# Three chained transformer blocks: kept products before two norms, a second router on unscaled rows, and block 3's biases, values and key weights on other queues

## The chip, the cores and the metric

One NeuronCore of one Trainium2 chip runs the whole program; the other cores are idle. The time is device microseconds of one execution. Shown are 3 runs of the kernel before, and one more execution under the hardware profiler, which gives the trace. TensorE is PE below, VectorE DVE, ScalarE ACT, GpSimd POOL and SyncE SP.

## The reference

Sequence 512, width 1024, batch 1, everything in float32. Block 1 is a hybrid mixer, a cross attention on 512 memory rows and a hierarchical mixture of experts; block 2 has differential, window and memory attention on one projection and an expert-choice feed-forward; block 3 has neighbourhood and latent attention and a SwiGLU. What the change touches, cut to the core:

```
def rms_norm(x, gain):
    return x * lax.rsqrt(jnp.mean(x * x, -1, keepdims=True) + EPS) * gain

def expert_choice_ffn(h, w_router, w_gate, w_up, w_down):   # h = rms_norm(x, ffn_norm_g_2)
    aff = jax.nn.softmax(h @ w_router, axis=-1)             # 512 x 16
    g, idx = lax.top_k(swapaxes(aff, 1, 2), cap)            # the 64 best rows of each expert
    xe = h[idx]
    ye = (silu(xe @ w_gate) * (xe @ w_up)) @ w_down         # 16 experts
    return zeros_like(h).at[idx].add(ye * g[..., None])

def memory_attention(q, mk, mv):                            # block 2
    return softmax(q @ mk.T * scale) @ mv

def neighbourhood_attention_2d(q, k, v, rpb):               # block 3: 8 rows x 64 columns, 8 heads
    s = q @ k_nb.T * scale + rpb_cols[:, row_bias_idx]      # bias by the distance in rows and columns
    return softmax(s) @ v_nb
```

## The kernel before, in words

It is one program for one core, written with tile pools; a scheduler orders each engine's instructions when the program is built, and inserts the waits. Nothing is reordered at run time: an instruction that waits holds up all behind it on its engine, and a DMA issue that waits holds up its engine's queue.

A float32 product is made of three fast ones: each operand is split into a high part (wh, xh: a cast on ACT, line 218) and a low part (wl, xl: a subtraction on DVE, line 221), and PE adds high by high, low by high and high by low. Weights come in groups of 4 x 128 rows by 512 columns (raw, 1 MB) through SP's queue (raw_group, line 340). dense_tiles (line 367 issues its matmuls) works through the four token tiles of 128 rows for a first use; dense (line 419) holds four accumulators and runs over k.

*out_proj* (line 282) runs token tiles 0 and 1, then 2 and 3. In each pass it goes over k, splits two halves of 512 output columns, and multiplies for both tiles in turn. Both tiles of a pass so end together; finish then adds to the residual h (line 311) and calls the norm of the next step.

*Block 2's router* (moe2_tile, router_T, line 883 on): DVE multiplies the residual by the norm's gain (L883, 128x512 twice a tile), PE transposes (L433), copies go to SBUF (L438, L436), PE multiplies by the router weights (L894), and the softmax takes the row factor r in. The transposed affinities (L1582) of four tiles then go through 8 rounds of MAX8 and MATCH_REPLACE on DVE (L1594, L1595), 8 rows of each expert a round. Beside each round keep_warm issues one small matmul and 5 of 128x128 on PE (L191, L193). From the replaced places the positions follow (L1600 to L1604), PE transposes them (L1607), DVE builds one-hot tiles, PE gathers each expert's rows (L1625), and the experts run (L1662 gate and up, L1693 down), with weights streamed into all free room. For each pair of experts two broadcasts of positions and affinities (L1669) serve the later scatter.

*Block 2's memory attention* consists of parts of two heads and 256 queries: scores (L828) into PSUM, softmax on DVE and ACT (L456 to L476), transposes (L836), copies (L839), and for every two parts value products (L1393). The scheduler puts them between the matmuls of block 2's projections (L419).

*Block 3's neighbourhood attention* (mixer3): values v are projected first (line 1765), written row tile by row tile to DRAM (vd, L1766) and read back in eight windows (vw, L1785). Queries and keys follow. The position bias is read as overlapping rows (rv, L1794), which come mirrored; a matmul with the anti-diagonal matrix turns them (L1797), and DVE adds the mask (L1802). The vd, vw and rv transfers are on ACT's queue, between its casts.

## Time and profile before

| what | value |
|---|---|
| median of 3 runs | 3418.66 us (3416.3 to 3419.46) |
| profiled execution | 3424.08 us |
| its span | 3422.2 us |
| TensorE clock granted, mean | 0.983 |
| PE / DVE / ACT / POOL busy | 95% / 48% / 38% / 4% |
| DMA moved | 713.96 MB, mean 209 GB/s |

Busy shares are averages over stages with different limits, and a busy PE is modelled from issue to end, so back-to-back matmuls show longer than their spacing. The profiled execution is 5.4 us above the median of the runs. [...]

### The profile page before, as it was taken

How to read it: one execution, taken by the hardware profiler on the slowest of the kernel's cores; microseconds unless marked ns; L12 is line 12 of the kernel's file. 1: busy time of each engine (PE TensorE's matmuls, PEld its weight loads, DVE VectorE, ACT ScalarE, POOL GpSimd, SP SyncE). 2: the span in 40 equal slices, each digit the busy share in tenths (PEclk: the TensorE clock that was granted, in tenths of full speed). 3: DMA queues.
4: the chain of work that ended last, by engine and by line, in shares of the span. 5: the costliest groups of instructions: out<-in, count | busy, mean ns of one | idle time of the engine just before them, and what ended most of it. 6: DMA issues, size and time to landing. Idle time of an engine off the chain costs nothing.

```text
span 3422.2 us, 41346 instructions
## 1 busy us (share of the span) xinstructions
PE 3242.2 (95%) x15500; PEld 2092.0 (61%) x15500; DVE 1636.8 (48%) x3520; ACT 1289.1 (38%) x2662; POOL 130.4 (4%) x128
## 2 busy tenths in 40 slices
PE   8999989998999999999999998898888999999998
PEld 6777866667767767668634333232224676788886
DVE  5546789998354454656311111011014446573356
ACT  6334658886344353554100000000003344452244
POOL 0010010002000000000000000000000000000000
PEclk9999989999999999999899999999999999999999
DMA  5115479985112212114799999999997312133243
GB/s 169 58 62 141 148 261 376 373 313 199 62 50 72 73 53 87 50 35 171 269 402 420 422 420 422 421 421 423 420 422 272 98 50 68 62 99 99 80 165 137
DMA packets 212938, 713.96 MB, mean 209 GB/s; under 512 B 20144, under 2 KB 28096, under 8 KB 180352
## 3 DMA queue, kind: packets, MB, share of 16 engines
q1 hardware_dynamic: 190272, 668.38, 51.1%
q10 hardware_dynamic: 19520, 32.43, 3.0%
q0 software_dynamic: 2944, 10.49, 1.0%
q8 instruction: 123, 2.02, 0.2%
q14 instruction: 79, 0.65, 0.1%
HBM read 693.68 MB, written 17.56 MB: 208 GB/s over the span
## 4 chain that ended last, share of the span: by engine, by line
PE 75%; DMA 13%; DVE 6%; ACT 2%; issue 1%; POOL 1%; ACTq 0%; SPq 0%; POOLq 0%; DVEq 0%
PE acc L419 23%; PE acc L1662 8%; PE acc L282 7%; PE acc L1085 5%; PE acc L1277 5%; PE acc L1693 3%; PE acc L1107 2%; PE pst L433 2%; DMA xl<-in_w_exp_up_dram 2%; DMA rawx<-in_w_exp_gate_dram 2%; DMA xl<-in_w_exp_down_dram 2%; PE sc L1625 2%; PE acc L367 2%; DMA rawx<-in_w_exp_down_dram 2%; DVE wl L221 1%
## 5 line engine op out<-in xcount | busy, mean ns | idle before, releaser
L221 DVE TENSOR_TENSOR wl<-raw,wh 128x512 fp32r<-128x512 f32 (+3 forms) x910 | 606.6, 683 | 578.0 <-ACT wh L218 525.1
L218 ACT CAST wh<-raw 128x512 fp32r<-128x512 f32 (+3 forms) x910 | 546.5, 612 | 737.8 <-PE acc L419 491.4
L419 PE MATMUL acc<-xh,wh 128*128 128x512 f32 x1072 | 426.4, 398 | 7.1 <-ACT wh L218 5.0
L419 PE MATMUL acc<-xl,wh 128*128 128x512 f32 x1072 | 425.0, 396 | 0.0
L419 PE MATMUL acc<-xh,wl 128*128 128x512 f32 x1072 | 424.4, 396 | 0.0
L1662 PE MATMUL acc<-rawx,xe 128*64 128x512 f32 x1256 | 293.0, 601 | 29.3 <-DMA rawx<-in_w_exp_up_dram 20.9
L419 PEld LDWEIGHTS acc<-xh,wh 128*128 128x128 f32 x1072 | 202.2, 189 | 61.0 <-issue 10.2
L419 PEld LDWEIGHTS acc<-xl,wh 128*128 128x128 f32 x1072 | 202.4, 189 | 51.5 <-issue 13.2
L419 PEld LDWEIGHTS acc<-xh,wl 128*128 128x128 f32 x1072 | 202.2, 189 | 50.4 <-issue 10.8
L1662 PEld LDWEIGHTS acc<-rawx,xe 128*64 128x64 f32 x1256 | 84.2, 137 | 228.2 <-issue 147.7
L1693 PE MATMUL acc<-rawx,wh 128*64 128x512 f32 x640 | 147.0, 599 | 13.1 <-DMA rawx<-in_w_exp_down_dram 13.0
L282 PE MATMUL acc<-wl,xsh 128*128 128x512 f32 x336 | 132.9, 396 | 4.8 <-DVE wl L221 4.7
L207 POOL TENSOR_TENSOR pw_r<-pw_v,halfneg 128x1 f32<-128x1 f32 (+2 forms) x64 | 58.4, 913 | 2053.8 <-DVE pw_v L206 2036.2
L282 PE MATMUL acc<-wh,xsl 128*128 128x512 f32 x336 | 132.2, 394 | 0.0
L282 PE MATMUL acc<-wh,xsh 128*128 128x512 f32 x336 | 128.7, 392 | 0.0
L1662 PE MATMUL acc<-raw,xe 128*64 128x512 f32 x512 | 119.2, 598 | 9.6 <-DMA raw<-in_w_exp_gate_dram 9.6
L1681 DVE SCALAR_TENSOR_TENSOR wl<-wl,acc 128x512 f32<-128x512 f32 x32 | 22.0, 687 | 205.0 <-PE acc L1662 205.0
L468 ACT ACTIVATE e<-e,smx 128x512 f32<-128x512 f32 (+3 forms) x160 | 98.7, 618 | 50.1 <-DVE smx L466 37.3
L438 ACT COPY wh<-pst 128x512 f32<-128x512 f32 x32 | 18.7, 585 | 260.1 <-PE pst L433 260.0
L1693 PEld LDWEIGHTS acc<-rawx,wh 128*64 128x64 f32 x640 | 42.1, 136 | 103.7 <-issue 68.5
L1085 PE MATMUL acc<-wh,xeh 128*96 128x512 f32 x256 | 103.6, 406 | 0.7 <-ACT xeh L218 0.7
L1085 PE MATMUL acc<-wl,xeh 128*96 128x512 f32 x256 | 103.6, 404 | 0.0
(538 smaller groups left out, 5581.3 us busy)
## 6 DMA issues: line engine op xcount, KB each, us to landing
rawx<-in_w_exp_up_dram SPq DMA_DIRECT2D x80, 1024.0 KB
rawx<-in_w_exp_down_dram SPq DMA_DIRECT2D x80, 1024.0 KB
rawx<-in_w_exp_gate_dram SPq DMA_DIRECT2D x77, 1024.0 KB
raw<-in_w_in_dram SPq DMA_DIRECT2D x58, 1024.0 KB
raw<-in_w_exp_gate_dram SPq DMA_DIRECT2D x34, 1024.0 KB
raw<-in_w_exp_down_dram SPq DMA_DIRECT2D x32, 1024.0 KB
raw<-in_w_exp_up_dram SPq DMA_DIRECT2D x30, 1024.0 KB
raw<-in_w_ffn_out_dram SPq DMA_DIRECT2D x22, 1024.0 KB
```

The lines of the kernel that those rows point to most:

```text
L218: nc.scalar.copy(hi, src)
L221: nc.vector.tensor_sub(lo, src, hi.bitcast(F32))
L282: nc.tensor.matmul(acc[a, hf], l[:, js], r, start=(k == 0 and q == 0), stop=(k == nk - 1 and q == 2))
L367: self.nc.tensor.matmul(acc[a], l[:, k, js], r[:, :n], start=(k == 0 and q == 0), stop=(k == nk - 1 and q == 2))
L419: nc.tensor.matmul(outs[j], l, r, start=(kk == 0 and q == 0), stop=(kk == nk - 1 and q == 2))
L433: nc.tensor.transpose(pt[:, k * P:(k + 1) * P], src[:, (b + k) * P:(b + k + 1) * P], self.ident)
L468: nc.scalar.activation(es[i], src[i], AF.Exp, bias=nm[:, i:i + 1], scale=sc[i], accum_out=l[:, i:i + 1])
L1085: nc.tensor.matmul(ps, l[:, k], r, start=(k == 0 and q == 0), stop=(k == 7 and q == 2))
L1107: nc.tensor.matmul(py[hf], l[:, k], r, start=(k == 0 and q == 0), stop=(k == 3 and q == 2))
L1277: nc.tensor.matmul(acc[j], l[:, js], r, start=(k == 0 and q == 0), stop=(k == nk - 1 and q == 2))
L1662: nc.tensor.matmul(acc[f // 2][f % 2 * 64:(f % 2 + 1) * 64], cur[:, k, es], raw[f], start=(k == 0), stop=(k == 7))
L1693: nc.tensor.matmul(py[hf * 64:(hf + 1) * 64], uT[ab][:, kk, c * 64:(c + 1) * 64], raw[:, d, hf * 512:(hf + 1) * 512], start=(i + d == 0), ...
```

## The change

1. out_proj gets keep=True for w_out (block 1) and w_out_2 (block 2): in the pass of tiles 2 and 3, the products of the last two k are held back, and issued for tile 2, then for tile 3, each right ahead of that tile's finish.
2. Block 2's router transposes h itself. The norm's gain is multiplied into the router weights once, at the start of the program: a new load fgain (128x8x1 of float32, from ffn_norm_g_2) stands on ACT's queue behind the load of those weights, and a new DVE multiply (line 1353 of the changed kernel) waits for both. The scaled rows hn (ACT, h times r) are written after the router; the gathered rows xe are multiplied by the gain where they were copied. The load of the gain as a full row goes.
3. The last of the 8 top-k rounds issues 1 matmul to keep PE busy, in place of 5.
4. The first pair's broadcasts (L1669) are issued behind expert 0's gate products.
5. The mirrored bias is written once to DRAM (rpb_d) by eight DRAM-to-DRAM copies on SP's queue, early in block 2, behind a weight load; rv is read from there, already turned, and the anti-diagonal matmul and its matrix go. rv, vd and vw are issued from POOL. The key weights (columns 512 to 1023) are loaded ahead into the room of the later merged tile, and the weights of values and queries are loaded ahead too.

The diff, cut:

```
@@ -262,7 +262,7 @@
-    def out_proj(self, W, nk, get, upd, after):
+    def out_proj(self, W, nk, get, upd, after, keep=False):
@@ -270,18 +270,30 @@
+            kept = []
...
+            def products(a, k, hf, x, w):
+                js = slice((a - tiles[0]) * P, (a - tiles[0] + 1) * P)
+                for q, (l, r) in enumerate(((0, 0), (0, 1), (1, 0))):
+                    nc.tensor.matmul(acc[a, hf], x[l][:, js], w[r], start=(k == 0 and q == 0),
+                                     stop=(k == nk - 1 and q == 2))
...
                     raws[k // 2] = load(k)
-                xh, xl = get(k, tiles[0] * P)
+                x = get(k, tiles[0] * P)
                 for hf in range(2):
-                    wh, wl = self.wsplit(raws[k // 2][:, k % 2, hf * 512:(hf + 1) * 512], 512)
-                    for i, a in enumerate(tiles):
-                        js = slice(i * P, (i + 1) * P)
-                        for q, (l, r) in enumerate(((xh, wh), (xh, wl), (xl, wh))):
-                            nc.tensor.matmul(acc[a, hf], l[:, js], r, start=(k == 0 and q == 0),
-                                             stop=(k == nk - 1 and q == 2))
+                    w = self.wsplit(raws[k // 2][:, k % 2, hf * 512:(hf + 1) * 512], 512)
+                    if keep and tiles[0] and k >= nk - 2:
+                        kept.append((k, hf, x, w))
+                    else:
+                        for a in tiles:
+                            products(a, k, hf, x, w)
...
             def finish(a):
+                for b in kept:
+                    products(a, *b)
                 for hf in range(2):
@@ -342,7 +354,7 @@
-        self.nc.sync.dma_start(v, W[k0 * P:(k0 + g) * P, c0:c0 + n].rearrange("(g p) n -> p g n", p=P))
+        self.loaded = self.nc.sync.dma_start(v, W[k0 * P:(k0 + g) * P, c0:c0 + n].rearrange("(g p) n -> p g n", p=P)).ins
@@ -784,7 +796,7 @@
         self.out_proj(I["w_out"], 8, lambda k, t0: (yh[:, k, t0:t0 + 256], yl[:, k, t0:t0 + 256]), self.add_h,
-                      lambda a: self.norm_tile(a, g, yh, yl))
+                      lambda a: self.norm_tile(a, g, yh, yl), keep=True)
         return yh, yl
@@ -1337,6 +1349,8 @@
         nc.scalar.dma_start(self.rw, I["w_router_2"].rearrange("(k p) e -> p k e", p=P))
+        nc.scalar.dma_start(self.fgain, I["ffn_norm_g_2"].rearrange("o (k p) -> p (o k)", p=P))
+        nc.vector.tensor_mul(self.rw, self.rw, self.fgain.unsqueeze(2).to_broadcast([P, 8, 16]))
         Q = lambda: B.tile([P, S], F32, name="qkv", bufs=24)
@@ -1366,6 +1380,15 @@
+        self.rpb_d = self.dr.tile([8, P, 489], F32, name="rpb_d")
+        rpb = I["na_rpb_3"]
+        with tc.issue_after(self.loaded):
+            for r in range(8):
+                nc.sync.dma_start(self.rpb_d[:, r * 16:(r + 1) * 16, :],
+                                  bass.AP(tensor=rpb.tensor, offset=rpb.offset + 63 * (7 - r) + 15,
+                                          ap=[[945, 8], [-1, 16], [1, 489]]))
@@ -1550,7 +1573,8 @@
         with tc.tile_pool(name="m2x", bufs=1, reuse_waits="tile") as X:
-            self.out_proj(I["w_out_2"], 8, self.split_get(merged, 0.5, X, 2), self.add_h, self.moe2_tile)
+            self.out_proj(I["w_out_2"], 8, self.split_get(merged, 0.5, X, 2), self.add_h, self.moe2_tile,
+                          keep=True)
         self.KX.close()
@@ -1558,7 +1582,6 @@
         R = self.R = self.RX.enter_context(tc.tile_pool(name="moe2r", bufs=1, side="right", reuse_waits="tile"))
-        self.mg = self.row("ffn_norm_g_2")
         self.aff = R.tile([P, S], F32, name="aff")
@@ -1566,10 +1589,17 @@
         nc, R = self.nc, self.R
-        xt, r = self.router_T(a, self.hn[:, a])
+        h = self.h[:, a]
+        xt = []
+        for b in range(2):
+            xt.append(self.gate_tile().rearrange("p (k t) -> p k t", k=4))
+            self.transposes(xt[b], h[:, b * 512:(b + 1) * 512], 4, eng="v" if b else "a")
+        r = self.tile_rstd(h)
         yield
         js = slice(a * P, (a + 1) * P)
-        pl = self.router(xt, 16)
+        pl = self.acc()[:, :16]
+        for k in range(8):
+            nc.tensor.matmul(pl, xt[k // 4][:, k % 4], self.rw[:, k], start=(k == 0), stop=(k == 7))
         st = R.tile([P, 4], F32, name="st", bufs=2)
@@ -1580,6 +1610,7 @@
         nc.vector.tensor_copy(self.aff[:16, js], pt[:16, :P])
+        nc.scalar.activation(self.hn[:, a], h, AF.Copy, scale=r)
@@ -1594,7 +1625,7 @@
                 src = wk
-                self.keep_warm(m8[:16], 5)
+                self.keep_warm(m8[:16], 5 if i < 7 else 1)
@@ -1624,9 +1655,15 @@
                         b = slice(m + i, m + min(i + 4, g))
-                        (nc.scalar.copy if b.start % 2 else nc.vector.tensor_copy)(t[:, b], ps[:, i:min(i + 4, g)])
+                        if b.start % 2:
+                            nc.scalar.activation(t[:, m], ps[:, 0], AF.Copy, scale=self.fgain[:, m:m + 1])
+                        else:
+                            n = b.stop - b.start
+                            nc.vector.tensor_mul(t[:, b], ps[:, i:i + n],
+                                                 self.fgain[:, b].unsqueeze(2).to_broadcast([P, n, P]))
                     yield t
@@ -1659,16 +1696,19 @@
                         for f in range(4):
-                            nc.tensor.matmul(acc[f // 2][f % 2 * 64:(f % 2 + 1) * 64], cur[:, k, es], raw[f],
-                                             start=(k == 0), stop=(k == 7))
+                            mm = nc.tensor.matmul(acc[f // 2][f % 2 * 64:(f % 2 + 1) * 64], cur[:, k, es], raw[f],
+                                                  start=(k == 0), stop=(k == 7))
+                    if not pg:
+                        gated = mm.ins
                     pg.append(acc)
...
                     bp, bw = self.pst(), self.pst()
-                    for b, src in ((bp, pos), (bw, aff)):
-                        for d in range(2):
-                            nc.tensor.matmul(b[d * 64:(d + 1) * 64],
-                                             self.ident[:16, e + d:e + d + 1].to_broadcast([16, 64]), src[:16],
-                                             start=True, stop=True)
+                    with tc.issue_after(gated) if e == 0 else ExitStack():
+                        for b, src in ((bp, pos), (bw, aff)):
+                            for d in range(2):
+                                nc.tensor.matmul(b[d * 64:(d + 1) * 64],
+                                                 self.ident[:16, e + d:e + d + 1].to_broadcast([16, 64]), src[:16],
+                                                 start=True, stop=True)
                     ohT = self.np.tile([P, S], F32, name="nx", bufs=2)
@@ -1753,7 +1793,8 @@
         o_ml = [B.tile([P, S], F32, name=f"oml{i}") for i in range(4)]
-        merged = [B.tile([P, S], F32, name=f"m{i}") for i in range(8)]
+        room = B.tile([P, 8, S], F32, name="m")
+        merged = [room[:, i] for i in range(8)]
         self.g8 = B
@@ -1763,18 +1804,21 @@
             nc.vector.tensor_copy(t, ps)
-            nc.scalar.dma_start(vd[a * P:(a + 1) * P, :], t)
...
-        self.dense_tiles(W, 8, 1024, 512, xh, xl, ev_v)
-        anti = self.const("anti", N)
+            nc.gpsimd.dma_start(vd[a * P:(a + 1) * P, :], t)
...
+        raws = {c: [self.raw_group(W, kg, 4, c, 512) for kg in (0, 4)] for c in (1024, 0)}
+        for kg in (0, 4):
+            nc.sync.dma_start(room[:, kg:kg + 4], W[kg * P:(kg + 4) * P, 512:1024].rearrange("(g p) n -> p g n", p=P))
+        raws[512] = [room[:, kg:kg + 4] for kg in (0, 4)]
+        self.dense_tiles(W, 8, 1024, 512, xh, xl, ev_v, raws=raws[1024])
         nmask = self.const("nmask", N)
...
             q[j].rearrange("p (j r c) -> p j r c", j=4, r=8), ps.rearrange("p (r j c) -> p j r c", j=4, r=8),
-            AF.Copy, scale=0.125))
-        self.dense(W, 8, 512, 512, "T", xh, xl, lambda j, ps: nc.vector.tensor_copy(k[j], ps))
+            AF.Copy, scale=0.125), raws=raws[0])
+        self.dense(W, 8, 512, 512, "T", xh, xl, lambda j, ps: nc.vector.tensor_copy(k[j], ps), raws=raws[512])
         starts = (0, 8, 24, 32)
@@ -1782,22 +1826,18 @@
                 o = vd[(kk * 4) * 64 + starts[j]:, :]
-                nc.scalar.dma_start(t, bass.AP(tensor=o.tensor, offset=o.offset, ap=[[64 * 512, 4], [512, 32], [1, 512]]))
+                nc.gpsimd.dma_start(t, bass.AP(tensor=o.tensor, offset=o.offset, ap=[[64 * 512, 4], [512, 32], [1, 512]]))
                 row.append(t)
             vw.append(row)
-        rpb = I["na_rpb_3"]
...
                 rv = N.tile([P, 489], F32, name="rv", bufs=2)
-                nc.scalar.dma_start(rv, bass.AP(tensor=rpb.tensor, offset=rpb.offset + (2 * hp + hh) * 945,
-                                                ap=[[63, 8], [1, 16], [1, 489]]))
-                pb = self.pst()
-                nc.tensor.matmul(pb[:, :489], anti, rv, start=True, stop=True)
+                nc.gpsimd.dma_start(rv, self.rpb_d[2 * hp + hh])
                 tab = N.tile([P, 4, 8, 32], F32, name="tab", bufs=3)
                 for j, off in enumerate((16, 8, 8, 0)):
-                    w = pb[:, off:off + 7 * 63 + 32]
+                    w = rv[:, off:off + 7 * 63 + 32]
                     v = bass.AP(tensor=w.tensor, offset=w.offset, ap=[list(w.ap[0]), [63, 8], [1, 32]])
```

What it moves on the engines, at three places.

DVE at the kernel's start (xl: the low part of the first norm's transposed rows; wl: of the first weights; nx: the normed rows). Before:

```order
L541 CAST gmi<-c_gmask 128x256
L206 TENSOR_SCALAR pw_v<-ss 128x1
L231 SCALAR_TENSOR_TENSOR nx<-h,pw_r,grow 128x512 x2
L221 TENSOR_TENSOR xl<-pst,xh 128x4x128 x2
L206 TENSOR_SCALAR pw_v<-ss 128x1
L231 SCALAR_TENSOR_TENSOR nx<-h,pw_r,grow 128x512 x2
L221 TENSOR_TENSOR wl<-raw,wh 128x512 x2
L221 TENSOR_TENSOR xl<-pst,xh 128x4x128
```

Now:

```order
L553 CAST gmi<-c_gmask 128x256
L206 TENSOR_SCALAR pw_v<-ss 128x1
L231 SCALAR_TENSOR_TENSOR nx<-h,pw_r,grow 128x512 x2
L1353 TENSOR_TENSOR rw_8579<-rw_8579,fgain 128x128
L221 TENSOR_TENSOR xl<-pst,xh 128x4x128 x2
L206 TENSOR_SCALAR pw_v<-ss 128x1
L231 SCALAR_TENSOR_TENSOR nx<-h,pw_r,grow 128x512 x2
L221 TENSOR_TENSOR wl<-raw,wh 128x512 x2
L221 TENSOR_TENSOR xl<-pst,xh 128x4x128
```

The new multiply stands fourth in the rows now, ahead of the first xl.

PE in block 2, at the first parts of the memory attention (sc: scores, pst: transposes or value products, acc: the projection; L828, L836, L1393 and L419 are L840, L848, L1416 and L431 in the changed kernel). Before:

```order
L419 MATMUL acc<-xh,wl 128x512
L828 MATMUL sc<-kv,qkv 128x256 x4
L419 MATMUL acc<-xh,wh 128x512
L419 MATMUL acc<-xl,wh 128x512
L419 MATMUL acc<-xh,wl 128x512
L419 MATMUL acc<-xh,wh 128x512
L419 MATMUL acc<-xl,wh 128x512
L419 MATMUL acc<-xh,wl 128x512
L419 MATMUL acc<-xh,wh 128x512
L419 MATMUL acc<-xl,wh 128x512
L419 MATMUL acc<-xh,wl 128x512
L828 MATMUL sc<-kv,qkv 128x256 x4
```

Now:

```order
L431 MATMUL acc<-xh,wl 128x512
L840 MATMUL sc<-kv,qkv 128x256 x8
L848 MATMUL pst<-c_ident,xe 128x128 x4
L840 MATMUL sc<-kv,qkv 128x256 x4
L848 MATMUL pst<-c_ident,xe 128x128 x4
L1416 MATMUL pst<-gate,kv 128x512 x4
L840 MATMUL sc<-kv,qkv 128x256 x4
L848 MATMUL pst<-c_ident,xe 128x128 x8
L1416 MATMUL pst<-gate,kv 128x512 x4
L431 MATMUL acc<-xh,wh 128x512
```

Four parts that were spread between matmuls of the projection stand in one piece, about 97 rows earlier; four parts before had 3 to 9 projection matmuls between their steps.

ACT in block 3's first projections before (wh: the high parts of weights; vd: values to DRAM; vw: their windows), and POOL at the same place now (pw_r: norm factors; rv: bias rows). ACT before:

```order
L1785 DMA vw_19329<-vd 128x1x512
L218 CAST wh<-raw 128x512 x5
L1785 DMA vw_19333<-vd 128x1x512
L218 CAST wh<-raw 128x512
L1766 DMA vd<-nv 128x512
L1785 DMA vw_19337<-vd 128x1x512
L218 CAST wh<-raw 128x512
L1785 DMA vw_19341<-vd 128x1x512
L1785 DMA vw_19331<-vd 128x1x512
L1785 DMA vw_19335<-vd 128x1x512
L218 CAST wh<-raw 128x512
L1785 DMA vw_19339<-vd 128x1x512
```

POOL now:

```order
L207 TENSOR_TENSOR pw_r<-pw_v,halfneg 128x1 x6
L1837 DMA rv<-rpb_d 128x489 x2
L207 TENSOR_TENSOR pw_r<-pw_v,halfneg 128x1 x2
L1837 DMA rv<-rpb_d 128x489
L1807 DMA vd<-nv 128x512 x2
L1829 DMA vw_19316<-vd 128x1x512
L1829 DMA vw_19320<-vd 128x1x512
L1807 DMA vd<-nv 128x512
L1829 DMA vw_19324<-vd 128x1x512
L1829 DMA vw_19328<-vd 128x1x512
L1807 DMA vd<-nv 128x512
L1837 DMA rv<-rpb_d 128x489
```

On ACT, 25 casts of raw now follow each other here without a DMA issue between them.

## Rows read from the trace of the kernel before

**Rows 1.** The page's part 1: busy us, share of the span, instructions.
```profile
PE 3242.2 (95%) x15500; PEld 2092.0 (61%) x15500; DVE 1636.8 (48%) x3520; ACT 1289.1 (38%) x2662; POOL 130.4 (4%) x128
```

**Rows 2.** The page's part 4: the chain that ended last, by engine.
```profile
PE 75%; DMA 13%; DVE 6%; ACT 2%; issue 1%; POOL 1%; ACTq 0%; SPq 0%; POOLq 0%; DVEq 0%
```

**Rows 3.** Timeline of the kernel's start: start us, us, engine, line, what.
```profile
16.75 1.29 DVE L221 TENSOR_TENSOR xl<-pst,xh 128x512 fp32r<-128x512 f32 x2 [6.45 <-ACT xh L218]
...
20.74 0.78 PE L367 MATMUL acc<-wh,xh 128*128 128x512 f32 x1
```

**Rows 4.** DMA queues from 10 to 18.3 us: packets, MB, share of 16 engines.
```profile
q1 hardware_dynamic: 1292, 3.04, 93.0%
q10 hardware_dynamic: 1038, 0.07, 8.6%
```

**Rows 5.** DMA queues from 42.5 to 44 us.
```profile
q10 hardware_dynamic: 1040, 0.07, 47.7%
```

**Rows 6.** Timeline of one part of block 2's memory attention.
```profile
893.03 1.99 PE L828 MATMUL sc<-kv,qkv 128*128 128x256 f32 x8
...
897.25 0.62 DVE L476 TENSOR_SCALAR xe<-xe,smx 128x256 f32<-128x256 f32 x2
...
898.89 0.60 PE L836 MATMUL pst<-c_ident,xe 128*128 128x128 f32 x4
...
900.03 3.63 PE L1393 MATMUL pst<-gate,kv 128*128 128x512 f32 x8
```

**Rows 7.** Windows: stretch, length, busy us (instructions) by engine, PEclk, DMA share, GB/s.
```profile
375.00:380.00 5.00, 3.92 (x21) 2.73 (x19) 3.65 (x11) 2.19 (x6) 0.55 (x1) 1.00 1.03 388
895.00:900.00 5.00, 5.00 (x27) 3.87 (x26) 3.49 (x10) 2.27 (x7) 0.00 (x0) 1.00 0.01 5
1635.00:1640.00 5.00, 3.85 (x27) 2.83 (x25) 4.97 (x10) 2.91 (x6) 0.93 (x1) 1.00 0.76 218
1640.00:1645.00 5.00, 3.98 (x19) 3.87 (x19) 1.42 (x5) 2.89 (x5) 0.55 (x1) 0.51 1.00 395
1670.00:1675.00 5.00, 5.00 (x21) 2.03 (x22) 1.51 (x4) 0.59 (x1) 0.00 (x0) 0.92 0.00 0
1740.00:2600.00 860.00, 789.11 (x3512) 267.67 (x3508) 105.33 (x154) 47.66 (x81) 0.00 (x0) 1.00 1.02 421
2660.00:2670.00 10.00, 4.99 (x15) 3.64 (x15) 2.50 (x4) 2.18 (x4) 0.00 (x0) 0.70 0.38 117
2680.00:2760.00 80.00, 79.96 (x441) 51.85 (x439) 47.38 (x186) 36.71 (x99) 0.00 (x0) 1.00 0.17 52
```

**Rows 8.** Timeline of block 2's router and top-k.
```profile
1635.57 0.39 PE L282 MATMUL acc<-wl,xsh 128*128 128x512 f32 x1
...
1635.80 0.39 PE L282 MATMUL acc<-wh,xsl 128*128 128x512 f32 x1
...
1643.58 3.59 PE L894 MATMUL sc<-rw,gate 128*128 128x16 f32 x16 [1.02 <-ACT L L1577]
...
1649.59 0.28 DVE L1582 COPY aff<-pst 16x128 f32<-16x128 f32 x1 [0.56 <-PE pst L1581]
...
1664.53 0.41 DVE L1604 TENSOR_SCALAR pos<-pos 16x512 f32<-16x512 f32 x1
...
1669.63 0.42 PE L1607 MATMUL pst<-c_ident,pos 16*128 16x16 f32 x4
...
1673.92 2.58 PE L1662 MATMUL acc<-rawx,xe 128*64 128x512 f32 x6
```

**Rows 9.** Timeline of block 3's projections.
```profile
2639.79 0.98 PE L1797 MATMUL pst<-rv,c_anti 128*128 128x489 f32 x2
...
2647.26 10.27 ACTq L1785 DMA_DIRECT2D vw<-vd  x3
...
2665.93 2.18 ACT L218 CAST wh<-raw 128x512 fp32r<-128x512 f32 x4 [7.69 <-issue]
...
2666.60 0.80 PE L419 MATMUL acc<-xh,wh 128*128 128x512 f32 x1 [5.01 <-ACT wh L218]
```

2 lines of the change are left out of this document (1 added, 1 removed).

## The prediction

> **What bounds the kernel now.** I read the page first: TensorE is busy for 95% of the span [rows 1], and the chain that ended last is 75% PE and 13% DMA [rows 2]. So there is no single bound: in most stages PE is full, and an edit is worth what it takes from PE or from what PE waits for; in one stage the DMA engines are full. The stretches by windows say which is which. From 1740 to 2600 us (block 2's experts) the DMA share is 1.02 at 421 GB/s and PE has 789 of 860 us [rows 7]: there only an earlier start of the transfers counts. From 2680 to 2760 (block 3's neighbourhood attention) PE is busy 79.96 of 80 [rows 7]: every PE instruction taken away there counts in full. Then I read the timeline at the four places that the change touches: the start, block 2's memory attention, its router, and block 3's projections. The profiled execution took 3424.08 us (span 3422.2 and 1.9 around it); the median of the runs is 3418.66, 5.4 lower. The sum below is a difference, which I set against 3424.08 and carry over to the median. A measurement of this kernel can tell about 0.2%, 6.8 us, from no change.
>
> **1. Block 3: what leaves ACT's queue and PE.** Before, ACT issues the vw loads, and waits for the vd stores with them. One issue group stands at 2647.26 for 10.27 us; the casts (L218) behind it come late, the last after 7.69 us, and PE idles 5.01 us before 2666.60 [rows 9]. The granted clock is 0.70 over 2660 to 2670, PE busy 4.99 of 10 [rows 7]; the first matmul after the gap took 0.80 us [rows 9] where 0.39 is usual [rows 8], so PE stood at the half level. With the 5.0 us of idle go some 2 us of slow matmuls: **-7.0**. In the new order ACT has 25 casts in a row there. The sixteen L1797 matmuls go too; a pair took 0.98 us [rows 9], of which the second can have overlapped the first, so 0.41 to 0.49 each: 6.5 to 7.8 us. I take **-6.5**, since PE is full beside them. Against it: POOL now issues rv, vd and vw. Behind them on POOL stand two norm factors (L207) and later vd stores, whose nv buffer DVE's next copy needs. The first vw is needed only after two more projections. Nothing before shows POOL issuing these; if the same waits passed on in full the cost would be the 5.0 us gap again, if nothing is queued behind them nought. I take nought. The mask add (L1802) reads SBUF in place of PSUM and stays as it is. Range of the part: -7 to -15.
>
> [...]
>
> **2. Second router.** Before, the last product of w_out_2 is issued at 1635.80 and the last affinity is written at 1649.59, 13.8 us later [rows 8]; two tiles' gain multiplies, transposes and router products stand in that time one behind the other, the last router at 3.59 us. Now the last two k of tiles 2 and 3 are kept and tile 2's issued first: 12 products of tile 3 at 0.23 us spacing [rows 8], 2.8 us, run beside tile 2's norm and router. The eight 128x512 gain multiplies go. PE has some 2.5 us of tile 2's transposes and router ahead of tile 3's end, so that end moves to about 1638.3, and one tile's chain (half of 13.8) follows: affinity at 1645.2, **-4.4**. The eight top-k rounds on DVE are unchanged. PE's keep-warm matmuls run behind DVE: the position chain on DVE is over at 1665, the first PE instruction after them starts at 1669.63 [rows 8]. Fewer in the last round are worth 1.4 at most, I take **-1.0**; if the clock stayed full, the whole backlog of 4.7 could go. From there to the first expert matmul, 1673.92, are 4.3 us; the four broadcasts taken out ahead of it make it 3.2: **-1.1**. They run later in expert 0 instead, where PE is full. What counts is when the first weight buffer comes free: the DMA share is 0.00 in 1670 to 1675 with 1.02 from 1740 [rows 7], so the stage shifts as a whole. Sum **-6.5**; if the delayed broadcasts count fully, -4.5; if the clock stays up, -10.
>
> **3. Memory attention of block 2 in one piece.** This is a side effect: as the order shows, four parts (two heads) that stood between the matmuls of a projection now stand together. Before, the projection's matmuls filled every wait: from 895 to 900 PE is busy 5.00 of 5 [rows 7]. One part: scores begin at 893.03 (some 1.8 us of PE), the softmax on DVE and ACT ends with the multiply at 897.25 + 0.62, 4.84 after the scores' start; the value product (3.63) starts 1.14 after its transposes (898.89 to 900.03) [rows 6]. Walked through in the new order: after two parts' scores (3.6) PE waits 1.2 for the first softmax; before the first value product 0.7; then, with nothing but the third part's transposes to do, 2.6 for the fourth part's softmax, and 0.7 again. That is 5.2 us, **+5.5** with hand-overs. The least is 3 (the engines' order lets some of it overlap), the most about 10 if the clock falls for a few microseconds after.
>
> **4. The start.** The router weights are now multiplied by the gain on DVE (line 1353) right behind the first norm and ahead of the first xl, at 16.75 [rows 3], and the multiply waits for both loads. The weight load has 1024 rows of 64 B. From 10 to 18.3 us queue q10 moved 1038 packets and the SP queue q1 1292 [rows 4]: near one for one. So a row cost 8 us / 64 rows per engine = 0.125 us, and the load landed at about 18.3. Alone, 1040 such packets took 47.7% of 1.5 us [rows 5], 0.011 us each. The gain's load follows on the same queue with 1024 elements of 4 B. At 0.011 us it lands at 19.0, a delay of the first xl by 2.3 us; at 0.125 us at 26.3, a delay of 9.6. One for one with SP's packets (93.0% of 8.3 us x 16 / 1292 = 0.096 us, plus 0.011) it takes 6.8 us and lands at 25.1, 8.3 late. All that follows hangs on xl: the second tile's norm, the first wl, the first projection matmul at 20.74 [rows 3]. The delay is PE's idle time, and nothing behind gives it back, since PE is full from there. I take **+8.0**.
>
> [...]
>
> **5. The rest, at nothing.** The gain at the gathered rows replaces copies by multiplies of the same shape in the DMA-bound stage. The scaling of h moves behind the router; its reader, the first gather, comes 20 us later. The eight mirror copies follow an SP load whose successors wait for buffers anyway, while the DMA engines have room. In block 1 the kept products fill a boundary where PE already has the other tile's work.
>
> **Sum.** -7.0 - 6.5 - 6.5 + 5.5 + 8.0 = -6.5: 3417.6 for the profiled execution, **3412.2** for the median, -0.19%. That lies at the edge of what can be told.
>
> **Rivals.**
> *The start costs little* (the gain's load lands with the weights', or its elements go as longer runs): +2.3 in place of 8, sum -12.2, 3406.5. Against it stands the one-for-one sharing in rows 4. A full clock through the router gives nearly the same (-10 in place of -6.5).
> [...]
> *Slower: the clock falls in the memory attention.* Place: the new chunk, PE idle 5 of 21 us. Price: its 16 us of PE work at half clock take up to 16 us more, less the 5 of waits that this swallows, so +8 to +11. Point: the granted clock falls in its first third. For it: 1635 to 1640 has 3.85 of 5 us busy, and the next slice 0.51; against it: 375 to 380 has 3.92 of 5 and keeps 1.00 [rows 7]. Sum +1.5 to +4.5, 3420 to 3423; with the start at its upper bound and the router at its lower (+3.6 in all) 3427, slower.
>
> **How the numbers follow.** Forecast 0.54; its own spread of some 6 us splits it evenly between faster and same (0.27 each). Small start or full clock 0.19, all faster. No gain from the queue 0.09, same. Clock falls 0.18: 0.08 same, 0.10 slower. That makes faster 0.46, same 0.44, slower 0.10. The range takes in the rivals' times and both ends of the start and of block 3: 3398 to 3426.
>
> **What would show it.** Right: DVE's multiply at line 1353 starts about 25 us, and the first L367 matmul near 29; no PE gap over 1 us in block 3's query projection, and about sixteen fewer PE matmuls in neighbourhood attention; the first expert matmul some 6.5 us earlier against the router's last product block; four PE gaps of 0.7 to 2.6 us around the chunk. Wrong: the multiply before 20 us; a PE wait on an xh or wl after a POOL-issued DMA; a granted clock under 0.7 in the chunk; the expert stage ending no earlier although it began earlier.

## The result and the profile after

The changed kernel took **3440.64 us** (median of 4 runs, 3438.34 to 3442.18), the kernel before beside it 3417.48 (4 runs): 1.0066 times as long, 95% interval 1.0053 to 1.0078. That is 23 us slower, with an interval well clear of 1; the forecast was 3412.2, its range 3398 to 3426. The profiled execution of the changed kernel took 3439.67 us (span 3437.9), 15.6 more than the profiled one before, which lay 5.4 above its own median. Of the ten executions of experiment 2 below one was slow, 7586.26 us; its median of 3428.9 is of all ten, and without it 3428.68.

The page's part 1 answers to [rows 1]: PE is less busy than before, by 9.5 us, in a span that is 15.7 us longer. What was lost is waiting, by PE's own count.

```profile
PE 3232.7 (94%) x15476; PEld 2086.2 (61%) x15476; DVE 1632.2 (47%) x3513; ACT 1290.0 (38%) x2662; POOL 142.2 (4%) x148
```

To find where, I matched PE instructions of the two traces in the stage order and noted how much later the changed kernel starts each:

| place | after minus before, us |
|---|---|
| first projection matmul (20.74, now 27.61) | +6.9 |
| 806 us, ahead of block 2's memory attention | +5 |
| 941, behind it | +15 |
| 1635, before the second router | +18 |
| block 2's first expert matmul | +8 |
| 2600, end of the experts | +18 |
| the end | +16 |

So time is lost at the start, in the memory attention and inside the experts; the second router gives 10 us back; and block 3, which was to gain 13.5, gains 2. Most lines shifted by some 10 to 40: L367 is L379 now, L419 is L431, L282 is L279, L828 is L840, L1393 is L1416, L1662 is L1699, L1785 is L1829.

**The start.** The timeline answers to [rows 3]. DVE's multiply waits 13.85 us for the gain, and the first xl, which stood at 16.75, follows at 23.97.

```profile
6.97 0.59 ACTq L1352 DMA_DIRECT2D fgain<-in_ffn_norm_g_dram  x1
...
23.76 0.29 DVE L1353 TENSOR_TENSOR rw<-rw,fgain 128x128 f32<-128x128 f32 x1 [13.85 <-DMA fgain<-in_ffn_norm_g_dram]
23.97 1.28 DVE L221 TENSOR_TENSOR xl<-pst,xh 128x512 fp32r<-128x512 f32 x2
...
27.61 0.78 PE L379 MATMUL acc<-wh,xh 128*128 128x512 f32 x1
```

**Windows** (stretch, length, busy us by engine, granted share of the full PE clock, DMA share, GB/s), answering to [rows 7]. In the memory attention's chunk, 870 to 900, PE is busy for 21.9 of 30 us, where before it was full; in the experts the transfers run at 416 GB/s, before at 421, with the same DMA share of 1.02; in block 3's projections PE has 4.02 of 10 and then 6.97 of 10, at a DMA share of 1.04 and 0.81.

```profile
870.00:880.00 10.00, 6.30 (x30) 4.94 (x29) 3.04 (x10) 4.76 (x13) 0.00 (x0) 1.00 0.02 7
880.00:890.00 10.00, 8.11 (x32) 5.21 (x32) 3.85 (x11) 3.83 (x12) 0.00 (x0) 1.00 0.00 0
890.00:895.00 5.00, 3.68 (x8) 1.86 (x9) 1.21 (x4) 0.50 (x3) 0.00 (x0) 0.68 0.02 3
895.00:900.00 5.00, 3.81 (x10) 1.64 (x10) 1.54 (x3) 3.25 (x6) 0.00 (x0) 0.98 0.00 0
...
1740.00:2600.00 860.00, 784.18 (x3499) 267.60 (x3499) 105.85 (x155) 46.49 (x79) 0.00 (x0) 1.00 1.02 416
2660.00:2670.00 10.00, 4.02 (x18) 2.96 (x16) 2.09 (x4) 2.39 (x4) 1.44 (x3) 0.84 1.04 265
2670.00:2680.00 10.00, 6.97 (x23) 5.64 (x24) 5.20 (x11) 1.24 (x2) 4.18 (x7) 0.65 0.81 226
```

The kernel before, in the first two of these windows:

```profile
870.00:880.00 10.00, 10.00 (x46) 8.28 (x45) 2.77 (x4) 2.47 (x4) 0.00 (x0) 1.00 0.29 103
880.00:890.00 10.00, 10.00 (x46) 8.33 (x45) 2.38 (x4) 4.51 (x8) 0.00 (x0) 1.00 0.32 105
```

**What PE waits for** from 864 to 902 (line, tile, releaser: us in all, times, longest). The first row is a wait that the prediction did not have: the second and third part's scores (L840) wait until ACT's exp (L480) has read the scores of the part before.

```profile
PE sc L840 <- ACT xe L480: 3.7, 2, 2.1
PE pst L848 <- DVE xe L488: 2.3, 1, 2.3
PE acc L431 <- ACT wh L218: 1.2, 1, 1.2
PE pst L1416 <- ACT gate L851: 0.9, 2, 0.5
```

The order on PE was fixed when the program was built; the timeline of SP's queue shows what may have led to it. The eight mirror copies stood on it for 31 us, with the next weight loads behind them. Each copy is issued in 0.63 us (the median; 0.84 at most); what the later ones waited for the trace does not tell.

```profile
813.59 9.47 SPq L357 DMA_DIRECT2D raw<-in_w_in_dram  x2
823.11 31.36 SPq L1389 DMA_DIRECT2D rpb_d<-in_na_rpb_dram  x8
854.58 8.11 SPq L357 DMA_DIRECT2D raw<-in_w_in_dram  x4
```

**Block 3's projections**, answering to [rows 9]. The 5.01 us that PE waited for ACT's cast are gone, and PE waits 9.01 us for DVE instead. DVE's last copy into nv waits 10.20 us. There is one nv buffer, and the third vd store, which reads it, is issued on POOL at 2659.49, behind two vw loads and 1 us after its copy has ended; it has landed only when the last copy starts at 2672.28, 12.8 us after its issue. In the kernel before, the third store was issued on ACT at 2639.35, and the last copy started at 2644.71 without a wait for it.

```profile
2658.08 1.43 POOL L1829 DMA_DIRECT2D vw<-vd  x2 [2.37 <-PE acc L379]
2659.49 0.60 POOL L1807 DMA_DIRECT2D vd<-nv  x1
2660.07 1.37 POOL L1829 DMA_DIRECT2D vw<-vd  x2
...
2672.28 0.69 DVE L1806 COPY nv<-acc 128x512 f32<-128x512 f32 x1 [10.20 <-DMA vd<-nv]
...
2673.03 0.80 PE L431 MATMUL acc<-xh,wh 128*128 128x512 f32 x1 [9.01 <-DVE nv L1806]
```

**The router**, answering to [rows 8]: from the last product to the last affinity are 7.7 us now, 13.8 before; to the first expert matmul 26.5, before 38.1.

```profile
1655.49 0.39 PE L279 MATMUL acc<-wh,xsl 128*128 128x512 f32 x1
...
1663.19 0.28 DVE L1612 COPY aff<-pst 16x128 f32<-16x128 f32 x1 [0.56 <-PE pst L1611]
...
1681.97 1.94 PE L1699 MATMUL acc<-rawx,xe 128*64 128x512 f32 x8 [0.38 <-DVE xe L1665]
```

### The profile page after: what moved, and what is told of

It is laid out like the page before. It is cut to its first block, busy times and chain, and to the rows that moved or that the text cites. A ratio compares the mean times of both kernels' runs of the same rounds, so it can differ in the third digit from the quotient of the medians.

```text
span 3437.9 us, 41299 instructions
## 1 busy us (share of the span) xinstructions
PE 3232.7 (94%) x15476; PEld 2086.2 (61%) x15476; DVE 1632.2 (47%) x3513; ACT 1290.0 (38%) x2662; POOL 142.2 (4%) x148
## 4 chain that ended last, share of the span: by engine, by line
PE 54%; DMA 13%; DVE 4%; ACT 1%; issue 1%; POOL 1%; POOLq 0%; ACTq 0%; SPq 0%; DVEq 0%
PE acc L431 20%; PE acc L1699 7%; PE acc L279 5%; PE acc L1289 5%; DMA xl<-in_w_exp_up_dram 3%; PE acc L1733 3%; DMA rawx<-in_w_exp_gate_dram 3%; DMA xl<-in_w_exp_down_dram 3%; PE pst L445 2%; PE sc L1656 2%; DMA rawx<-in_w_exp_up_dram 1%; PE pst L1742 1%; DMA xl<-in_w_exp_gate_dram 1%; PE sc L1536 1%; DMA rawx<-in_w_exp_down_dram 1%; PE pst L1555 1%
## 5 line engine op out<-in xcount | busy, mean ns | idle before, releaser
L221 DVE TENSOR_TENSOR wl<-raw,wh 128x512 fp32r<-128x512 f32 (+1 forms) x902 | 599.7, 682 | 559.9 <-ACT wh L218 508.9
L218 ACT CAST wh<-raw 128x512 fp32r<-128x512 f32 (+1 forms) x902 | 541.7, 612 | 715.4 <-PE acc L431 488.2
L431 PE MATMUL acc<-xh,wh 128*128 128x512 f32 x1072 | 425.4, 397 | 12.2 <-DVE nv L1806 9.0
L431 PE MATMUL acc<-xl,wh 128*128 128x512 f32 x1072 | 424.5, 396 | 0.0
L431 PE MATMUL acc<-xh,wl 128*128 128x512 f32 x1072 | 423.9, 395 | 0.0
L1699 PE MATMUL acc<-rawx,xe 128*64 128x512 f32 x1256 | 292.0, 599 | 32.3 <-DMA rawx<-in_w_exp_up_dram 23.6
L431 PEld LDWEIGHTS acc<-xh,wh 128*128 128x128 f32 x1072 | 202.3, 189 | 66.5 <-issue 9.8
L431 PEld LDWEIGHTS acc<-xl,wh 128*128 128x128 f32 x1072 | 202.1, 189 | 51.8 <-issue 13.3
L431 PEld LDWEIGHTS acc<-xh,wl 128*128 128x128 f32 x1072 | 202.2, 189 | 49.2 <-issue 9.3
L1699 PEld LDWEIGHTS acc<-rawx,xe 128*64 128x64 f32 x1256 | 84.0, 136 | 230.7 <-issue 142.2
L279 PE MATMUL acc<-wl,xsh 128*128 128x512 f32 x336 | 133.1, 396 | 4.8 <-DVE wl L221 4.7
L279 PE MATMUL acc<-wh,xsl 128*128 128x512 f32 x336 | 132.9, 396 | 0.0
L279 PE MATMUL acc<-wh,xsh 128*128 128x512 f32 x336 | 129.9, 394 | 0.0
L1699 PE MATMUL acc<-raw,xe 128*64 128x512 f32 x512 | 119.2, 598 | 11.2 <-DMA raw<-in_w_exp_gate_dram 10.7
L480 ACT ACTIVATE e<-e,smx 128x512 f32<-128x512 f32 (+3 forms) x160 | 98.7, 618 | 50.1 <-DVE smx L478 37.3
```

Source lines behind the costliest of these rows:

```text
L218: nc.scalar.copy(hi, src)
L221: nc.vector.tensor_sub(lo, src, hi.bitcast(F32))
L279: nc.tensor.matmul(acc[a, hf], x[l][:, js], w[r], start=(k == 0 and q == 0), stop=(k == nk - 1 and q == 2))
L431: nc.tensor.matmul(outs[j], l, r, start=(kk == 0 and q == 0), stop=(kk == nk - 1 and q == 2))
L480: nc.scalar.activation(es[i], src[i], AF.Exp, bias=nm[:, i:i + 1], scale=sc[i], accum_out=l[:, i:i + 1])
L1699: mm = nc.tensor.matmul(acc[f // 2][f % 2 * 64:(f % 2 + 1) * 64], cur[:, k, es], raw[f], start=(k == 0), stop=(k == 7))
```

## The experiments

All times are medians; a ratio is against the kernel before run beside it, with its 95% interval. Unless another kernel is named, a gain is against the changed kernel's 3440.6. A gain is a difference of two medians, in part from different chips, and by the intervals good to some 3 to 7 us; where the ratios give a gain more than 2 us apart from it, that stands beside it.

**1. The start alone.** The multiply is put behind a small multiply on DVE that comes late in block 2, long after both loads.

```diff
-        nc.vector.tensor_mul(self.rw, self.rw, self.fgain.unsqueeze(2).to_broadcast([P, 8, 16]))
...
+        placed = nc.vector.tensor_mul(snk, snk, isl).ins
+        with tc.issue_after(placed):
+            nc.vector.tensor_mul(self.rw, self.rw, self.fgain.unsqueeze(2).to_broadcast([P, 8, 16]))
```

> The changed kernel with the DVE multiply of the router weights by the gain moved from the kernel's start into block 2 (behind the product of the sink logits); the gain's load stays where it is. Theory: the first xl waited for that load until 23.97 us against 16.75 before; the first xl comes back to about 16.8, the first projection matmul from 27.6 to about 20.7, and the time falls by 7 us, from 3440.6 to about 3433.6. Rival (a later stage that is bound by DMA absorbs a shift of the start): the first xl comes back but the time stays within 2 us of 3440.6.

Measured: 3430.95, 1.0037 [1.0023, 1.0052], a gain of 9.7. The first projection matmul starts 8.9 us earlier than in the changed kernel:

```profile
18.67 0.54 PE L379 MATMUL acc<-wh,xh 128*128 128x512 f32 x1
```

The load's wait is the start's whole loss, within what can be told. The matmul now starts 2 us ahead of the kernel before, which I did not follow up.

**2. The mirror copies alone.** Each of the eight is issued behind a weight load of its own, from the second set of block 2's query and key projections on.

```diff
+        if self.mirror:
+            with self.tc.issue_after(self.loaded):
+                self.mirror.pop(0)()
```

> The changed kernel with the eight mirror copies spread, one behind each of eight weight loads of block 2 from its second differential-attention half on, in place of all eight behind one load; the memory attention's parts then stand between the projection's matmuls as before the change. Theory: the 10 us by which the two traces drift apart between 806 and 941 us go (PE waits around 870 to 900 gone), and the time falls by 10 to about 3430.6. Rival (the drift is taken back later, in the experts' stage whose end the DMA sets): PE's waits go but the time stays at 3438 to 3441.

Measured: 3428.9, 1.0029 [1.0019, 1.0039], a gain of 11.7. The parts of the memory attention stand between the projection's matmuls again, and PE is full from 860 to 900:

```profile
860.00:900.00 40.00, 39.97 (x180) 32.95 (x178) 11.79 (x21) 14.10 (x27) 0.00 (x0) 1.00 0.33 105
```

The run shows that the copies' place on SP's queue made the chunk; the order and the loads' lateness were not tried apart.

**3. The vd stores alone, on ACT's queue again.**

```diff
-            nc.gpsimd.dma_start(vd[a * P:(a + 1) * P, :], t)
+            nc.scalar.dma_start(vd[a * P:(a + 1) * P, :], t)
```

> The changed kernel with the four stores of the values (vd) on ACT's queue again; their window loads (vw) and the bias rows (rv) stay on POOL. Theory A (the third store stood behind two window loads on POOL's queue, so the one nv buffer came free late): DVE's fourth nv copy no longer waits 10.2 us, PE's gap of 9.0 us before the query projection goes, and with the half clock after it the time falls by 9 to 11 us, to about 3430. Rival B (three weight loads on SP's queue at the same time make the stores slow, whatever queue they are on): the wait stays at 5 us or more and the time falls by 4 at most.

Measured: 3432.14, 1.0039 [1.0025, 1.0053], a gain of 8.5. What PE waits for from 2600 to 2720 begins with

```profile
PE acc L431 <- DVE nv L1806: 2.1, 1, 2.1
```

So 9.0 became 2.1. The stores no longer share a queue with the window loads, but there is still one buffer, and the view of nv shows that a store still takes up to 7.5 us to land:

```profile
DMA to landing us min/median/max: 3.3/5.4/7.5
```

DVE's last copy waits 3.36 us for it. Theory A holds in the main and rival B in part: weight loads run beside these stores too.

**4. The other repair of the same wait: two nv buffers**, all on POOL as in the change. This tells the buffer from the queue.

```diff
-            t = N.tile([P, 512], F32, name="nv")
+            t = N.tile([P, 512], F32, name="nv", bufs=2)
```

> The changed kernel with two nv buffers in place of one; vd, vw and rv all stay on POOL's queue in the same order. Theory (the wait is for the one buffer): DVE's wait of 10.2 us before the fourth nv copy goes or falls under 2 us, PE's gap of 9.0 us goes, and the time falls by 7 to 9 us as with vd on ACT's queue, to about 3432. Rival (POOL's queue: the stores come as late as before, and two buffers only move the wait, to the window loads' readers or to the fourth copy all the same): a DVE wait of 5 us or more remains and the time falls by 4 at most.

Measured: 3430.4, 1.0045 [1.0031, 1.006], a gain of 10.2 (7.2 by the ratios). The view of the tile nv, who waited for it (us, times), has POOL's instructions alone; DVE and PE are not in it:

```profile
POOL vw L1829: 5.7, 1
POOL vd L1807: 4.8, 2
...
DMA to landing us min/median/max: 2.6/5.3/10.3
```

POOL still waits, and a store still takes up to 10.3 us; it costs nothing once no copy waits for the landing. So the one buffer is what turned a slow store into a loss, and either repair will do. What makes the store slow on POOL's queue, the loads ahead of it or the way POOL issues, was not tried apart.

**5. The three repairs (1, 2, 3) together.**

> The three edits of the other runs together. If the three losses add up: 7 + 10 + 10 less than the changed kernel's 3440.6, about 3414, which is 3 us under the kernel before; the experts' stage then ends no earlier against the kernel before than its weights allow, so the router's gain of some 8 us is seen at the first expert matmul but not at the stage's end. Rival (the router's gain is kept once the rest is undone): 3403 to 3408.

Measured: 3410.67, 0.9978 [0.9967, 0.999], a gain of 30.0, and 9.7 + 11.7 + 8.5 = 29.9: three losses in different places, which add within what can be told (by the ratios 30.1 against 31.7). But the experts' transfers stayed at 417 GB/s:

```profile
1740.00:2580.00 840.00, 764.38 (x3390) 258.41 (x3386) 102.64 (x150) 45.30 (x77) 0.00 (x0) 1.00 1.02 417
```

**6. The kernel before again, with a profile**, on the chip of experiments 7 to 9, to see whether the 417 belongs to the chip or the moment.

> The kernel before, profiled once more. It tells whether the experts' stage is slower in the changed kernel or whether the first profile was another chip or moment: the first profile moved 421 GB/s from 1740 to 2600 us, the changed kernel and its three repaired versions 415 to 417. Theory S (it is something in the changed program): 420 to 423 GB/s here, too. Rival C (chip or moment): 415 to 417 GB/s here, and the stage takes some 10 us longer than in the first profile.

Measured: 3417.72, 1.0003 [0.9993, 1.0014]. It does not: here it is 421, and in experiment 8, on the same chip, 417.

```profile
1740.00:2580.00 840.00, 771.01 (x3430) 262.13 (x3426) 104.01 (x152) 46.49 (x79) 0.00 (x0) 1.00 1.02 421
```

**7. The copies alone**: the kernel before with the eight copies of experiment 2 added; nothing reads them.

> The kernel before with the eight mirror copies added, spread over block 2's weight loads, and read by nobody (block 3 reads its biases as before). It prices the copies alone, and tells whether 2 MB more in DRAM slow the experts' stage. If the copies are hidden: within 3 us of the kernel before. If the place in DRAM slows the stage (421 to 416 GB/s): 10 us slower and 416 GB/s in the profile.

Measured: 3417.82, 1.0006 [0.9996, 1.0015], and 421 GB/s. The copies are hidden, and are not what slows the experts.

**8. The router's part alone**, in the kernel before, with the multiply late as in experiment 1. The norm's gain, kept products, last keep-warm round and broadcasts are all in it.

```diff
+        self.fgain = self.cp.tile([P, 8], F32, name="fgain")
...
-                      lambda a: self.norm_tile(a, g, yh, yl))
+                      lambda a: self.norm_tile(a, g, yh, yl), keep=True)
...
```

> The kernel before with the router's part alone: kept products in both output projections, transposes of plain rows, the gain at the gathered rows, 1 in place of 5 matmuls in the last top-k round, broadcasts behind the gate products; the multiply of the weights by the gain in block 2, so that the start is not delayed. Block 3 is as before. Theory (the earlier start moves the whole DMA-bound stage): first expert matmul 8 to 13 us earlier, 7 to 10 us off the time, 3408 to 3411. Rival (the stage's end is set by the weights' bytes, which wait for buffers freed later, so an earlier start is given back): first expert matmul earlier by as much, the stage's end and the time within 3 us of the kernel before.

Measured: 3423.2, 1.0018 [1.0008, 1.0028]: slower than the kernel before, though its first expert matmul comes at 1663.36. In the kernel before that stood at 1673.92 [rows 8], in experiment 6 (the profile of the kernel before on this chip) at 1668.62. The part gains 5 us and more before the experts and loses more than that inside: matched as in the table above, PE is 7.8 us ahead of experiment 6 at 1700 and 3.4 behind at 2595, at 417 GB/s:

```profile
1740.00:2580.00 840.00, 764.40 (x3394) 258.92 (x3390) 102.67 (x151) 45.29 (x77) 0.00 (x0) 1.00 1.02 417
```

**9. Block 3's part alone**, in the kernel before, with the copies spread as in experiment 2 and vd on ACT.

> The kernel before with block 3's part alone: mirrored biases from DRAM (copies spread), key weights loaded ahead into the merged tile's room, rv and vw on POOL, vd on ACT. The router is as before. Theory: PE's 5.0 us gap at 2666, its slow matmuls and the sixteen anti-diagonal matmuls go: 10 to 13 us off, 3405 to 3408. Rival (the round trip through DRAM still holds something): 3 us off or less.

Measured: 3408.67, 0.9973 [0.9964, 0.9983], 8.1 faster than the kernel before, at 421 GB/s. Its largest wait on PE from 2600 to 2720 is again nv's:

```profile
PE acc L423 <- DVE nv L1776: 1.7, 1, 1.7
```

Matched with experiment 6, PE is 1.5 us ahead at 2640, 11.5 at 2800 and 7.1 at 3000. The 4.4 given back are not block 3's projections: from 2850 to 2900 the granted clock is 0.90 here and in the first profile of the kernel before, and 1.00 in experiment 6. So in its own place the part may be worth some 10.

**10. Nothing but 32 bytes.** What is left of the router's part that could touch the experts' transfers is the tile fgain, 32 bytes a partition. It moves by 32 bytes all that lies behind it on its side of SBUF: twelve of the sixteen 1 MB buffers that the experts' weights stream into. The other four (rawx in the pool rx) are allocated from the other side and stay. Here the kernel before gets a tile of that size that nobody uses.

```diff
+        nc.vector.memset(self.cp.tile([P, 8], F32, name="shift"), 0.0)
```

> The kernel before with one more tile of 32 bytes a partition, which nothing uses, where the change puts the gain's tile: every buffer behind it in that pool and in the pools after it lies 32 bytes further, as in the changed kernel, and nothing else differs. Theory P (the place of the weight buffers sets how long a packet takes: all kernels with the gain's tile show 4096- and 8192-byte packets longer by 1%): the experts' stage falls from 421 to 416 or 417 GB/s, and the time rises by 8 to 11 us, to about 3426. Rival O (the order or the pace of the transfers in the changed router slows them): 421 GB/s, and the time stays within 2 us of the kernel before.

Measured: 3426.81, 1.0023 [1.0014, 1.0033], 7.2 slower than the kernel before, with the experts at

```profile
1740.00:2580.00 840.00, 766.05 (x3402) 259.54 (x3398) 104.03 (x152) 46.49 (x79) 0.00 (x0) 1.00 1.02 417
```

This is the fourth loss. Matched with experiment 6, PE is 0.9 us ahead at 1700 and 8.4 behind at 2595, so the loss is made in the experts' stage.

**11. The router's part with fgain 256 bytes wide**, so that the buffers keep their place modulo 256.

```diff
-        self.fgain = self.cp.tile([P, 8], F32, name="fgain")
+        self.fgain = self.cp.tile([P, 64], F32, name="fgain")[:, :8]
```

> The router's part alone, with the gain's tile 256 bytes wide. With its 32-byte tile it was 6 us slower than the kernel before. Theory P: 421 GB/s, 8 to 11 us off its 3423.2, so 3412 to 3415, 2 to 5 us under the kernel before: the router's own gain. Rival O: 416 GB/s and 3423 again.

Measured: 3412.03, 0.9984 [0.9974, 0.9993], 7.6 faster than the kernel before (5.5 by the ratio), at 421 GB/s:

```profile
1740.00:2580.00 840.00, 769.80 (x3426) 261.62 (x3422) 104.06 (x152) 46.47 (x79) 0.00 (x0) 1.00 1.02 421
```

**12. The same without the kept products**, in blocks 1 and 2.

> The router's part alone with the wide gain's tile, but no products are kept in either output projection. The full router's part with the wide tile came to 3412.0. Theory (the forecast's step: the kept products let tile 2's router run beside tile 3's products, and with the gain's multiplies gone make 4.4 of 6.5 us): first expert matmul 2 to 4 us later than with kept products, and the time 2 to 4 us higher, 3414 to 3416. Rival (the gain is from the multiplies and the fewer matmuls in the last round alone): 3412 to 3413.

Measured: 3417.65, 1.0001 [0.999, 1.0013]. The last affinity is written 5.6 later than in experiment 11, and the run is 5.6 longer. Experiment 11 first, then this one:

```profile
1641.26 0.28 DVE L1606 COPY aff<-pst 16x128 f32<-16x128 f32 x1 [0.56 <-PE pst L1605]
...
1659.68 1.94 PE L1693 MATMUL acc<-rawx,xe 128*64 128x512 f32 x8 [0.38 <-DVE xe L1659]
```

```profile
1646.88 0.28 DVE L1605 COPY aff<-pst 16x128 f32<-16x128 f32 x1 [0.34 <-PE pst L1604]
...
1669.42 2.83 PE L1692 MATMUL acc<-rawx,xe 128*64 128x512 f32 x8 [0.38 <-DVE xe L1658]
```

The first expert matmul comes 9.7 later, where 2 to 4 were expected, and the two profiled executions are 10.4 apart (3407.54 and 3417.96), so 5.6 may be low. Part of the 9.7 is the clock: it is granted at 0.50 from 1645 to 1660 here, and at 0.53 and 0.78 from 1640 to 1650 in experiment 11, then at 1.00. By the medians the other edits of the part (no gain multiplies, a shorter last round, later broadcasts) are together worth some 2, which is within what can be told. Block 1's kept products were not tried apart from block 2's; PE in experiment 11 is 0.2 us ahead of this one at 700 us and even with it at 1600, so block 2's are what counts.

**13. The three repairs and the wide fgain.**

> The version with the three repairs, and the gain's tile made 256 bytes a partition wide in place of 32, so that the weight buffers behind it start at multiples of 256 bytes again as in the kernel before. Theory P: 421 GB/s in the experts' stage and 8 to 11 us off its 3410.7, about 3401. Rival O: 416 GB/s and the same time.

Measured: 3400.38, 0.9946 [0.9929, 0.9962], 10.3 less than experiment 5, at 421 GB/s:

```profile
1740.00:2580.00 840.00, 770.15 (x3428) 262.02 (x3426) 104.07 (x152) 46.47 (x79) 0.00 (x0) 1.00 1.02 421
```

**14. The changed kernel with the wide fgain alone.**

> The changed kernel with the gain's tile 256 bytes a partition wide in place of 32, and nothing else. Theory (the four losses add up): 420 to 421 GB/s in the experts' stage and 9 to 11 us off 3440.6, about 3431. Rival (the stage has slack that other losses use up): 3436 or more.

Measured: 3433.8 (3426.59 to 3437.16), 1.0043 [1.0027, 1.006], a gain of 6.8 at 420 GB/s:

```profile
1740.00:2580.00 840.00, 775.70 (x3485) 268.61 (x3482) 105.22 (x154) 45.87 (x78) 0.00 (x0) 1.00 1.01 420
```

That is below what was expected; its runs lie 10 us apart, so the place is worth 7 to 11 by experiments 10, 11, 13 and 14 together.

**15. All buffers of the experts at multiples of 256 bytes.** In the kernel before, and with the wide fgain, the ten buffers rawx lie 32 or 160 bytes past one. Two gaps, 96 and 32 bytes, move them.

```diff
+        nc.vector.memset(R.tile([P, 8], F32, name="gap_r"), 0.0)
...
+            nc.vector.memset(M.tile([P, 24], F32, name="gap_m"), 0.0)
```

> all3_pad with two more unused gaps (96 bytes in the pool of the experts' stage, 32 bytes at the other side of SBUF), so that the ten buffers named rawx start at multiples of 256 bytes too; in the kernel before and in all3_pad they start 32 or 160 bytes behind one, and only the six others of the stage are at a multiple. Theory P: all packets as short as the shortest, 309 ns for 8192 bytes against a mean of 311.4, so about 424 GB/s and some 6 us under all3_pad, about 3395. Rival (only the shift of the six matters, or the DRAM side sets the rest): within 2 us of all3_pad.

Measured: **3392.24**, 0.9925 [0.9908, 0.9942], 27.4 faster than the kernel before and the best of all. Its four runs (3390.84 to 3394.76) lie clear of the four of experiment 13 on the same chip (3398.07 to 3401.92).

```profile
1740.00:2580.00 840.00, 774.72 (x3452) 264.15 (x3448) 104.01 (x152) 46.47 (x79) 0.00 (x0) 1.00 1.02 425
```

## Why the prediction was wrong

The miss is 3440.6 - 3412.2 = 28.4 us. By the prediction's steps:

| step | forecast | measured | by experiment | miss |
|---|---|---|---|---|
| 1, POOL's queue and the nv buffer | 0 | +8.5 to +10.2 | 3, 4 | +8.5 to +10.2 |
| no step: the buffers' place | 0 | +7 to +11 | 10, 11, 13, 14 | +7 to +11 |
| 3, memory attention in one piece | +5.5 | +11.7 | 2 | +6.2 |
| 1, the rest of block 3 | -13.5 | -8.1 | 9 | +5.4 |
| 4, the start | +8.0 | +9.7 | 1 | +1.7 |
| 2, second router | -6.5 | -7.6 | 11 | -1.1 |
| sum | | | | 27.7 to 33.4 |

**The step that failed first: "I take nought"** in step 1. It had the mechanism in sight: it named the norm factors and "later vd stores, whose nv buffer DVE's next copy needs" as queued behind the new loads on POOL, and as the upper end "the 5.0 us gap again". But it argued from when vw is first needed, and not from when the store that sets nv free would land. With one buffer DVE's next copy waited for that landing. The store was issued in time, but among the vw loads on POOL it took 12.8 us to land, on ACT (experiment 3) at most 7.5; DVE waited 10.20 us and PE 9.01. The upper end was too low too: ACT's wait had been 10.27 [rows 9], and only the part of it that PE saw was carried over. The chance of no gain from the queue was put at 0.09; the move cost 8.5 to 10. The trace stands on both sides of the move: 10.27 us of wait on ACT before [rows 9], 9.01 on PE after. What changed with the queue is what stood behind what.

**What no step had: where the weight buffers lie.** Step 5 took "the rest, at nothing", and I read the new tile fgain as a load and never as 32 bytes ahead of most weight buffers. Step 2 even said what this stage is bound by (transfers, DMA share 1.02), so any price on those transfers counted in full: 7 to 11 us, as much as the router's whole gain. Experiment 10 shows it by itself, and 11 and 13 take it back.

**Step 3 was right in kind and half the size.** The waits forecast were the softmax's, 5.2 us; the trace has 3.2 of them (2.3 and 0.9). A weight's cast adds 1.2. The 3.7 us for the scores tile are missing in my walk: I let the parts' scores run one behind the other, while there is one scores buffer and a part must wait for the exp of the part before. The clock did fall as the rival had it, to 0.68 from 890 to 895 after two windows with 6.30 and 8.11 of 10 us busy, but late in the chunk and not in its first third: one value product (the eight L1416 matmuls from 892.04) at 5.25 us where it takes 3.63 [rows 6]. The waits sum to 8.1, and the whole is 11.7, above the step's "about 10". The rival's price, +8 to +11 for the term, came nearest, by a cause that was the smaller part.

**Step 1's gains** were 8.1 of 13.5 with the queue repaired. Some 1.7 to 2.1 of the rest is the nv wait that stays on ACT's queue too. The other 3 or so may be no loss at all: by the trace of experiment 9 the part gains 10 in its own place. The sixteen matmuls and the gap were not tried apart.

**Step 4 was right**: the gain landed at 23.76 at the latest, between its ends of 19.0 and 26.3 and nearer the one-for-one estimate (25.1). That the load goes as one packet for each of its 1024 elements, as the +8.0 takes it, was my own estimate, and no run before the change shows it. The trace after bears it out: up to 45 us the queue moves 1216 packets of 4 bytes, before 208, and 890 of them go from 17 to 23 us, and the multiply starts 16.8 us after the load's issue.

**Step 2 was right** in sum, 7.6 for 6.5, once the buffers' place was repaired. Of its terms the kept products gave 5.6 (forecast 4.4), the others 2 or nothing. The first expert matmul came 11.6 us nearer to the last product than in the first profile of the kernel before (26.5 for 38.1), but 7.1 nearer than in experiment 6 (33.6), where 6.5 was forecast. The clock makes the difference: it was granted at 0.50 to 0.51 from 1640 to 1660 in the first profile, and at 0.81, 0.50, 0.66 and then 1.00 in the 5 us windows from 1640 on in experiment 6. The changed kernel has 0.50 from 1660 to 1670, so the clock did not stay up as the upper end had it.

**In step 5** the copies are indeed hidden by the DMA engines' room (experiment 7: 1.0006). "Follow an SP load whose successors wait for buffers anyway" was wrong of the queue: all eight behind one load, the copies stood on SP's queue for 31 us, and this place of theirs made the piece of step 3 (experiment 2).

## What to carry to other kernels

When a DMA that waits moves to another queue, write down that queue's next instructions and ask which buffer each of them sets free: here one buffer, whose store had to land among POOL's loads, turned the move into a new wait, 10.20 us on DVE and 9.01 on PE. Ask of every step made longer or put together how many buffers the result has, not only how long it takes; one scores buffer made 3.7 us of wait here. And where a stage is bound by transfers, look at where a new small tile puts the big ones, and at GB/s in that stage before judging anything else: here a tile of 256 bytes left 420 to 421 GB/s, one of 32 bytes 416 to 417.
